# Gate projection of all but the first 272 tokens moved into the attention, between the heads

## The chip, the cores and the metric

The kernel runs on one core of a Trainium2 chip. The metric is the device time of one execution in microseconds (us), as the median of several runs. The core has five engines that run side by side and wait for each other by semaphores: TensorE (PE; PEld is its loading of weights, which lies beside its matmuls), VectorE (DVE), ScalarE (ACT), GpSimd (POOL) and SyncE (SP, whose queue issues nearly all transfers here, one after another in order).

## What is computed

Two layers over 2064 tokens (16 learned meta tokens, then 2048), width 1024. The change lies in the first, a sliding-window attention; the second, a gated DeltaNet, is untouched by it. Of the first:

```python
def attention_mixer(h, norm_w, w_in, q_norm_w, k_norm_w, sinks, w_out):
    u = rms_norm(h, norm_w) @ w_in
    q, k, v, gate = jnp.split(u, [ATTN_WIDTH, ATTN_WIDTH + ATTN_KV_WIDTH, ATTN_WIDTH + 2 * ATTN_KV_WIDTH], axis=-1)
    ...
    o = banded_sink_attention(q, k, v, sinks)
    return (o * jax.nn.silu(gate)) @ w_out
```

q has 16 heads of 64, k and v two; the gate has 1024 columns. A query sees the 128 latest keys, the meta tokens and a sink.

## The kernel before

All matmuls of the first layer run in the float32r format on operands split into a high and a low part, three matmuls for each product (mm3, lines 61 to 63: high by high, low by high, high by low).

**First stage, attn_proj.** The tokens are cut into 17 tiles (16 meta tokens, then 16 of 128). y_tile loads a tile of x, normalises it (norm_rows), transposes it and keeps the parts y_hi and y_lo in SBUF, in five chunks of 400, 384, 384, 384 and 512 tokens. load_w brings 256 columns of w_in and splits them. For q, k and v the tokens are the stationary operand: column blocks 0 and 1 together over all tiles, then 2, 3 and 4 (tile ps_mm). Then hook sets up constants. Then the gate, with the weights stationary and the tokens moving: for each of 8 column tiles of 128 and each chunk 24 matmuls into ps_g, a Silu on ACT (line 231), and a store to the DRAM tensor gate. q and kv go to DRAM too.

**Second stage, attention.** It goes by slots: slot j is a tile t and a group hg of four heads. scores(t, hg) makes s_ps (lines 393, 394), adds the distance table and takes the maximum on DVE (line 395), Exp on ACT (line 405), and scales on POOL. values(t, hg) follows four slots later: it transposes the meta part (tm) and the band (pt), splits them (ph on ACT, pl on DVE, line 444), multiplies by v (pv), multiplies by the gate on POOL (line 461) and splits into oh and ol. finish(t) multiplies by w_out (ps_o), adds x on DVE (line 476) and stores h1 (line 477). prep(t + 1) loads q and kv and transposes them (kps, qps).

```python
        for j in range(len(slots) + LAG):
            with tc.high_priority(offset=150 + (1000 if j < 12 else 0)):
                ...
                    scores(t, hg)
            with tc.high_priority(offset=250 + (1000 if j < 12 else 0)):
                ...
                    values(t, hg)
            for _ in range(2):
                next(fin, None) if fin else None
```

The framework orders the instructions of every engine ahead of time: it takes those that it reckons ready, by the order in which the code makes them, and a higher priority counts as if an instruction had been made that much earlier. On the chip every engine then keeps to its order. A pool gives each tag a number of buffers (bufs); a tile waits until the buffer's last reader is done.

**Second layer.** dn_proj begins where the last tiles of h1 are done; then dn_scan.

Of the kernel before, what the change touches and what calls it, by code (L numbers as in the profile page):

```python
# [15 lines left out]
P = 128  # L16
# [17 lines left out]
NV = 16  # L34
CW = 4096
# [71 lines left out]
def attn_proj(tc, a, sc, ident, hook):  # L107

    nc = tc.nc
# [3 lines left out]
    with (  # L113
# [7 lines left out]
        tc.tile_pool(name="p1w", reuse_waits="tile", bufs=2) as wp,  # L121
# [89 lines left out]
        for cc in range(2, 5):  # L211
            w = load_w(cc)
            for m, r0, i in tiles:
                qkv_tile([(cc, w)], m, r0)
        hook(tpp)
        for c0 in (5, 7):
            ws = [load_w(c0), load_w(c0 + 1)]
            cols = [(e, ct) for e in range(2) for ct in range(2)]
            if c0 == 5:
                order = [(e, ct, c) for e, ct in cols for c in ych]  # L220
            else:
                order = [(e, ct, ych[4]) for e, ct in cols[:0]] + [(e, ct, c) for c in ych[:4] for e, ct in cols]
                order += [(e, ct, ych[4]) for e, ct in cols[0:]]
            for e, ct, (t0, n, hi, lo) in order:
                wh, wl = ws[e]
                ps = mgp.tile([P, 512], F32, tag="mm", name="ps_g")
                for k in range(KT):
                    mm3(nc, ps[:, :n], wh[:, k, ct * P:(ct + 1) * P], wl[:, k, ct * P:(ct + 1) * P],
                        hi[:, k, :], lo[:, k, :], k == 0, k == KT - 1)
                st = sp.tile([P, 512], F32, tag="st", name="st_g")  # L230
                nc.scalar.activation(st[:, :n], ps[:, :n], AF.Silu)
                nc.sync.dma_start(sc["gate"][(c0 - 5 + e) * 2 + ct, :, t0:t0 + n], st[:, :n])


def attn_consts(tc, a, sc, ident, kp, tpp):
# [4 lines left out]
    for kind in range(3):  # L240
        di = kp.tile([P, 512], I32, tag="tmp", name="dist_i")
# [48 lines left out]
def attention(tc, a, sc, ident, ac):  # L290
    nc = tc.nc
    v = nc.vector
    with (
        tc.tile_pool(name="p2q", reuse_waits="tile", bufs=2) as lq,
        tc.tile_pool(name="p2s", reuse_waits="tile", bufs=4) as sp,
        tc.tile_pool(name="p2k", reuse_waits="tile", bufs=2) as lk,
        tc.tile_pool(name="p2p", reuse_waits="tile", bufs=5) as lx,
# [7 lines left out]
        tc.tile_pool(name="p2pt", reuse_waits="tile", bufs=2, space=PSUM) as tpp,  # L305
# [18 lines left out]
        def load_wout():  # L324
            for k in range(KT):
                for c in range(2):
                    raw = lk.tile([P, 512], F32, tag="wraw", name="wo_raw")
# [7 lines left out]
        def prep(t):  # L335
# [9 lines left out]
            else:  # L345
                kps = tpp.tile([P, 2, P], F32, tag="tp", bufs=2, name="kps")
                for kvh in range(2):
                    nc.tensor.transpose(kps[:, kvh, :], kv[:, kvh * P:(kvh + 1) * P], ident)
                kwin = lk.tile([P, 4, 272], F32R, tag="kwin", bufs=3, name="kwin")
# [12 lines left out]
            qst = lk.tile([P, AH, P], F32R, tag="qst", name="qst")  # L362
            for half in range(2):
                qps = tpp.tile([P, 4, P], F32, tag="tp", bufs=2, name="qps")
                for j in range(4):
                    nc.tensor.transpose(qps[:, j, :n], qt[:n, (half * 4 + j) * P:(half * 4 + j + 1) * P], ident[:n, :n])
                qv = qst[:, half * 8:half * 8 + 8, :].rearrange("p (j e) q -> p j e q", e=2)
# [6 lines left out]
            gt = lp.tile([P, KT, P], F32, tag="gate", bufs=1, name="gate_t")  # L374
            nc.sync.dma_start(gt[:, :, :n], sc["gate"][:, :, r0:r0 + n].rearrange("k p t -> p k t"))
            ctx[t] = dict(n=n, i=i, r0=r0, qst=qst, kwin=kwin, vt=vt, gt=gt)
            yield

        def scores(t, hg):
# [6 lines left out]
            for hh in range(4):  # L386
# [5 lines left out]
                q = c["qst"][:, hg * 4 + hh, :n]  # L392
# [27 lines left out]
        def values(t, hg):  # L420
# [4 lines left out]
            tm = tpp.tile([P, P], F32, tag="tp", bufs=2, name="tm")  # L425
# [28 lines left out]
            if hg == 0:  # L454
                c["xt"] = xp.tile([P, D], F32, tag="x", name="x_t")
                nc.sync.dma_start(c["xt"][:n], x_rows(a, i))
                c["oh"] = lp.tile([P, KT, P], F32R, tag="oh", name="oh")
                c["ol"] = lp.tile([P, KT, P], F32R, tag="ol", name="ol")
            ks = slice(hg * 2, hg * 2 + 2)
            oh, ol = c["oh"][:, ks, :n], c["ol"][:, ks, :n]  # L460
            nc.gpsimd.tensor_tensor(ot[:, :, :n], ot[:, :, :n], c["gt"][:, ks, :n], op=ALU.mult)
# [3 lines left out]
        def finish(t):  # L465

            c = ctx[t]
            n, r0, oh, ol, xt = c["n"], c["r0"], c["oh"], c["ol"], c["xt"]
            for cc in range(2):
                cs = slice(cc * 512, cc * 512 + 512)  # L470
                ps = pp.tile([P, 512], F32, tag="o", bufs=1, name="ps_o")
# [4 lines left out]
                v.tensor_tensor(xt[:n, cs], ps[:n], xt[:n, cs], op=ALU.add)  # L476
            (nc.gpsimd if t >= NXT else nc.sync).dma_start(sc["h1"][r0:r0 + n, :], xt[:n])
            yield

# [13 lines left out]
        LAG = 4  # L493
        for j in range(len(slots) + LAG):
            with tc.high_priority(offset=150 + (1000 if j < 12 else 0)):
# [9 lines left out]
            with tc.high_priority(offset=250 + (1000 if j < 12 else 0)):  # L505
# [8 lines left out]
            for _ in range(2):  # L514
                next(fin, None) if fin else None
        for _ in fin:
# [3 lines left out]
def dn_consts(tc, a, kp, ident, psum):  # L520
# [29 lines left out]
    nc.gpsimd.dma_start(nw, a["dn_norm_w"][0].rearrange("(k p) -> p k", p=P))  # L550
    cwr = kp.tile([P, P], F32, tag="cw_raw", name="cw_raw")
    nc.gpsimd.dma_start(cwr, a["dn_conv_w"][0].rearrange("k (t p) -> (k t) p", p=P))
# [8 lines left out]
    for h in range(2):  # L561
        b = slice(h * 64, h * 64 + 64)
        nc.gpsimd.dma_start(nA[b], a["dn_a_log"][0][h::2].unsqueeze(0).to_broadcast([64, 8]))
        nc.gpsimd.dma_start(dtb[b], a["dn_dt_bias"][0][h::2].unsqueeze(0).to_broadcast([64, 8]))
# [696 lines left out]
def body(tc, a, out, upto=9, dbg=None):  # L1261
    nc = tc.nc
    with (
# [7 lines left out]
        def dt(name, shape):  # L1271
# [66 lines left out]
```

## Time and profile before

| | us |
|---|---|
| median of 3 runs | 3198.64 |
| lowest and highest | 3197.79, 3203.32 |
| profiled execution | 3194.22 |
| its span in the trace | 3192.2 |

The trace is of one execution, so sums of its rows are held against 3194.22, of which 3192.2 is the span and 2.0 lies around it. Times within the span are counted from its start. A matmul's duration in the trace holds its pipeline's fill too, so PE's pace is read from the starts of matmuls that follow each other. In a row of a group, the last part is the idle time of the engine just before its instructions, with what ended most of it.

### The profile page before, as it was taken

Reading aid. Unit: us, or ns where it says so; the run is one execution under the profiler, and the core shown is the slowest. Engines: PE = TensorE matmul, PEld = TensorE weight load, DVE = VectorE, ACT = ScalarE, POOL = GpSimd, SP = SyncE. Lnnn points to the kernel's source line nnn. Section 1 sums busy time; section 2 is a strip of 40 time slices with the busy share of each in tenths; the row PEclk is TensorE's granted clock in tenths of the full one; section 3 lists DMA queues with packets and bytes.
Section 4 is the critical chain, followed back from the end, with each engine's and each line's share of the span. In section 5 each row is a group of like instructions: output and inputs, shape, how many; then the busy total and the mean of one; then the engine's idle time right before and its main releaser. Section 6 shows DMA issues by size and latency. Waiting matters only on the chain.

```text
span 3192.2 us, 54290 instructions
## 1 busy us (share of the span) xinstructions
PE 2988.6 (94%) x18685; PEld 2634.1 (83%) x18685; DVE 2228.9 (70%) x6092; ACT 1489.8 (47%) x4247; POOL 968.8 (30%) x1118
## 2 busy tenths in 40 slices
PE   7999998988888999988999999999999999999899
PEld 6999996766666999988999999989986777777687
DVE  6785029999897767896744777987238777788632
ACT  5414147776665444353323544342246665566421
POOL 3001004555453332231111323222145444444100
PEclk9999999999999999999999999999999999999999
DMA  5323123222223353545543444366555666555442
GB/s 120 102 67 98 62 83 95 74 81 65 72 71 102 88 131 92 138 111 144 158 120 80 111 124 124 98 156 186 131 151 159 182 184 177 170 172 163 155 139 99
DMA packets 553596, 385.92 MB, mean 121 GB/s; under 512 B 245513, under 2 KB 505353, under 8 KB 546153
## 3 DMA queue, kind: packets, MB, share of 16 engines
q1 hardware_dynamic: 517032, 365.05, 40.4%
q10 hardware_dynamic: 35952, 16.80, 1.9%
q0 software_dynamic: 336, 0.60, 0.4%
q8 instruction: 148, 2.42, 0.3%
q14 instruction: 128, 1.04, 0.1%
HBM read 245.38 MB, written 136.97 MB: 120 GB/s over the span
## 4 chain that ended last, share of the span: by engine, by line
PE 59%; DVE 23%; ACT 6%; DMA 6%; issue 4%; POOL 1%; SPq 1%; ACTq 0%; DVEq 0%; POOLq 0%
PE ps_d L61 6%; PE ps_d L63 6%; PE ps_d L62 6%; PE ps_o L61 4%; PE ps_o L62 4%; PE ps_o L63 4%; DVE acc L769 3%; PE r_ps L1150 3%; PE ds_ps L1177 3%; PE ps_mm L63 2%; PE ps_mm L61 2%; PE ps_mm L62 2%; DVE Xt L936 2%; PE o_ps L1181 2%; PE vn_ps L1166 2%
## 5 line engine op out<-in xcount | busy, mean ns | idle before, releaser
L61 PE MATMUL ps_d<-y_hi,wi_hi 128*128 128x384 f32 (+2 forms) x2304 | 755.3, 328 | 37.0 <-ACT u L761 30.8
L62 PE MATMUL ps_d<-y_lo,wi_hi 128*128 128x384 f32 (+2 forms) x2304 | 743.8, 323 | 0.0
L63 PE MATMUL ps_d<-y_hi,wi_lo 128*128 128x384 f32 (+2 forms) x2304 | 743.7, 323 | 0.0
L61 PEld LDWEIGHTS ps_d<-y_hi,wi_hi 128*128 128x128 f32 x2304 | 441.0, 191 | 52.1 <-ACT u L761 36.1
L63 PEld LDWEIGHTS ps_d<-y_hi,wi_lo 128*128 128x128 f32 x2304 | 440.9, 191 | 3.5 <-issue 3.3
L62 PEld LDWEIGHTS ps_d<-y_lo,wi_hi 128*128 128x128 f32 x2304 | 441.0, 191 | 3.2 <-issue 2.9
L640 POOL TENSOR_TENSOR wi_raw<-wi_raw,nw 128x1024 f32<-128x1024 f32 x96 | 211.1, 2199 | 685.2 <-DMA wi_raw<-in_dn_w_in 519.9
L769 DVE SCALAR_TENSOR_TENSOR acc<-u,cw,acc 128x1040 f32<-128x1040 f32 (+1 forms) x192 | 291.7, 1519 | 6.1
L57 DVE TENSOR_TENSOR wi_lo<-wi_raw,wi_hi 128x1024 fp32r<-128x1024 f32 x96 | 120.2, 1252 | 206.1 <-ACT wi_hi L56 187.3
L1152 POOL TENSOR_TENSOR S<-S,eL 128x256 f32<-128x256 f32 x248 | 157.2, 643 | 192.3 <-PE r_ps L1150 132.8
L61 PE MATMUL ps_o<-wo,oh 128*128 128x512 f32 x512 | 208.8, 408 | 3.7 <-ACT oh L56 2.9
L63 PE MATMUL ps_o<-wo,ol 128*128 128x512 f32 x512 | 204.1, 399 | 0.0
L1159 ACT ACTIVATE qs<-r_ps,ea 64x128 f32<-64x128 f32 x512 | 182.8, 363 | 44.3 <-DVE xp L1157 34.2
L62 PE MATMUL ps_o<-wo,oh 128*128 128x512 f32 x512 | 202.7, 396 | 0.0
L63 PE MATMUL ps_mm<-w_hi,y_lo 128*128 128x256 f32 (+1 forms) x680 | 192.5, 286 | 4.9 <-DVE y_lo L104 4.8
L61 PE MATMUL ps_mm<-w_hi,y_hi 128*128 128x256 f32 (+1 forms) x680 | 192.9, 286 | 3.0 <-DVE st L190 2.4
L1157 DVE SCALAR_TENSOR_TENSOR xp<-r_ps,c,bv_t 64x128 f32<-64x128 f32 x512 | 174.6, 343 | 27.6 <-ACT qs L1159 10.8
L761 ACT COPY u<-ps_d 128x384 f32<-128x384 f32 (+2 forms) x192 | 84.9, 442 | 232.1 <-PE ps_d L63 231.7
L62 PE MATMUL ps_mm<-w_lo,y_hi 128*128 128x256 f32 (+1 forms) x680 | 192.5, 285 | 0.0
L1150 PE MATMUL r_ps<-S,kq_t 128*128 128x256 f32 x512 | 160.5, 401 | 3.9 <-ACT qs L1159 3.5
L405 ACT ACTIVATE p<-p,nb 128x272 f32<-128x272 f32 (+2 forms) x272 | 134.0, 495 | 51.1 <-DVE nb L400 50.6
L56 ACT CAST wi_hi<-wi_raw 128x1024 fp32r<-128x1024 f32 x96 | 100.5, 1047 | 122.5 <-PE ps_d L62 101.5
(311 smaller groups left out, 7146.5 us busy)
## 6 DMA issues: line engine op xcount, KB each, us to landing
wi_raw<-in_dn_w_in SPq DMA_DIRECT2D x96, 512.0 KB, 4.1
kq_t<-d_kq SPq DMA_DIRECT2D x33, 512.0 KB, 5.3
bv_t<-d_bv SPq DMA_DIRECT2D x33, 512.0 KB, 5.2
x_t<-in_x SPq DMA_DIRECT2D x32, 512.0 KB, 3.7
d_kq<-kq SPq DMA_DIRECT2D x16, 1024.0 KB, 5.4
d_bv<-bv SPq DMA_DIRECT2D x32, 512.0 KB, 4.9
kt_t<-d_ktok SPq DMA_DIRECT2D x64, 256.0 KB, 4.1
z_t<-d_z SPq DMA_DIRECT2D x16, 1024.0 KB, 8.2
```

The lines of the kernel that those rows point to most:

```text
L56: nc.scalar.copy(hi, src)
L57: nc.vector.tensor_tensor(lo, src, hi.bitcast(F32), op=ALU.subtract)
L61: nc.tensor.matmul(ps, lhsT=lh, rhs=rh, start=start, stop=False)
L62: nc.tensor.matmul(ps, lhsT=lh, rhs=rl, start=False, stop=False)
L63: nc.tensor.matmul(ps, lhsT=ll, rhs=rh, start=False, stop=stop)
L405: nc.scalar.activation(p4[:n, hh, k0:272], p4[:n, hh, k0:272], AF.Exp, bias=nb[:n, hh:hh + 1], scale=SLOPES[hg * 4 + hh], accum_out=z[:n, ...
L640: nc.gpsimd.tensor_tensor(raw, raw, nw.unsqueeze(2).to_broadcast([P, KT, P]), op=ALU.mult)
L769: v.scalar_tensor_tensor(acc[:, :ncol], in0=u[:, j:j + ncol], scalar=cw[:, ct, j:j + 1], in1=acc[:, :ncol], op0=ALU.mult, op1=ALU.add)
L1150: nc.tensor.matmul(r, lhsT=kq[:, g, :], rhs=S[:, g], start=True, stop=True)
L1152: nc.gpsimd.tensor_tensor(S[:, g], S[:, g], pers["eL"][hf][:, :, g, n].unsqueeze(2).to_broadcast([P, 2, P]), op=ALU.mult)
L1157: v.scalar_tensor_tensor(xp[hb[h]], in0=r[0:64, h, :], scalar=pers["c1"][hf][hb[h], g, n:n + 1], in1=bv[hb[h], g, :], op0=ALU.mult, op1=AL ...
L1159: nc.scalar.activation(qs[hb[h]], r[64:128, h, :], AF.Copy, scale=pers["ea"][hf][hb[h], g, n:n + 1])
```

## The change

The gate of the first 272 tokens (the meta tile and two more) stays in the first stage (gate_first), between the column blocks, which are taken in the order 2, 5, 3, 6, 4, 7, 8. For the other 1792 tokens, the parts of the normalised tokens (gy) and of the gate's weights (gw) are stored to DRAM in the first stage. In the attention a generator, gates, works through 56 units (7 chunks of 256 tokens by 8 column tiles) of two halves of 12 matmuls, loads gw (512 KB a half) and gy (1 MB a half chunk) from DRAM two halves ahead, takes a Silu and stores the gate. The loop takes its steps between the slots, at the plain priority. To make room, the transposes have one PSUM buffer instead of two, and other tiles shrink or lose a buffer: the gate is loaded for each slot, x and h1 in halves of 512 columns. The small constants' loads of the second layer go from POOL's queue to SP's.

```diff
@@ y_tile
             norm_rows(nc, sp, xp, xt, m)
             transpose_split(nc, tpp, ident, xt, m, hi, lo, c0)
+            if r0 >= G0:
+                ci, off = divmod(r0 - G0, GN)
+                for hl, y in enumerate((hi, lo)):
+                    nc.sync.dma_start(sc["gy"][ci, :, :, hl, :, off:off + m],
+                                      y[:, :, c0:c0 + m].bitcast(F32).rearrange("p (h k) t -> p h k t", h=2))
@@ attn_proj, behind the first pass (wp has bufs=3 in place of 2)
-        for cc in range(2, 5):
-            w = load_w(cc)
-            for m, r0, i in tiles:
-                qkv_tile([(cc, w)], m, r0)
-        hook(tpp)
-        for c0 in (5, 7):
-            ws = [load_w(c0), load_w(c0 + 1)]
...
+        def gate_first(e, w):
+            wh, wl = w
+            hi, lo = at[0][:2]
+            for ct in range(2):
+                cs = slice(ct * P, ct * P + P)
+                for hl, x in enumerate((wh, wl)):
+                    nc.sync.dma_start(sc["gw"][e * 2 + ct, :, :, hl],
+                                      x[:, :, cs].bitcast(F32).rearrange("p (h k) c -> p h k c", h=2))
                 ps = mgp.tile([P, 512], F32, tag="mm", name="ps_g")
                 for k in range(KT):
+                    mm3(nc, ps[:, :G0], wh[:, k, cs], wl[:, k, cs], hi[:, k, 0:G0], lo[:, k, 0:G0], k == 0, k == KT - 1)
...
+        order = [2, 5, 3, 6, 4, 7, 8]
+        ws = {}
+        for j, cc in enumerate(order):
+            for c in order[j:j + 2]:
+                if c not in ws:
+                    ws[c] = load_w(c)
+            if cc < 5:
+                for m, r0, i in tiles:
+                    qkv_tile([(cc, ws[cc])], m, r0)
+                if cc == 4:
+                    hook(tpp)
+            else:
+                gate_first(cc - 5, ws[cc])
@@ attention
+        tc.tile_pool(name="p2g", reuse_waits="tile", bufs=3) as gyp,
-        tc.tile_pool(name="p2pt", reuse_waits="tile", bufs=2, space=PSUM) as tpp,
+        tc.tile_pool(name="p2pt", reuse_waits="tile", bufs=1, space=PSUM) as tpp,
...
+        def gates():
+            units = [(ci, ct) for ci in range(NGC) for ct in range(KT)]
+            ys, wts = {}, {}
+            gps = pp.tile([P, 2, GN], F32, tag="g", bufs=1, name="ps_g")
+            for u, (ci, ct) in enumerate(units):
+                ps = gps[:, u % 2, :]
+                for kh in range(2):
+                    nu = u * 2 + kh
+                    for w in (nu, nu + 1, nu + 2):
+                        if w // 2 < len(units) and w not in wts:
+                            c2, t2 = units[w // 2]
+                            y = (c2, w % 2)
+                            if y not in ys:
+                                ys[y] = gyp.tile([P, 2, 4, GN], F32R, tag="gy", name="gy")
+                                nc.sync.dma_start(ys[y].bitcast(F32), sc["gy"][c2, :, w % 2])
+                            wts[w] = gyp.tile([P, 2, 4, P], F32R, tag="gw", name="gw")
+                            nc.sync.dma_start(wts[w].bitcast(F32), sc["gw"][t2, :, w % 2])
+                    y, w = ys[ci, kh], wts.pop(nu)
+                    for k in range(4):
+                        mm3(nc, ps, w[:, 0, k], w[:, 1, k], y[:, 0, k], y[:, 1, k], kh + k == 0, kh + k == 4)
+                        if k == 1:
+                            yield
+                    if kh == 0:
+                        yield
+                st = gyp.tile([P, GN], F32, tag="st", bufs=2, name="st_g")
+                nc.scalar.activation(st, ps, AF.Silu)
+                t0 = G0 + ci * GN
+                nc.sync.dma_start(sc["gate"][ct, :, t0:t0 + GN], st)
+                yield
@@ the loop over slots (offsets 200 and 330 in place of 150 and 250)
+        filler, gdone = gates(), 0
...
+            while gdone * (len(slots) - 7) < NGC * KT * 4 * (j + 1) and next(filler, 1) is None:
+                gdone += 1
```

How the order of the instructions changes, at three places. On PE, around a tm (the transposes of the meta part) in the middle of the attention, before:

```order
L61 MATMUL ps_o<-wo_hi_6032,oh 128x512
L62 MATMUL ps_o<-wo_lo_6033,oh 128x512
L426 MATMUL tm<-ident,px 128x128
L63 MATMUL ps_o<-wo_hi_6032,ol 128x512
L61 MATMUL ps_o<-wo_hi_6034,oh 128x512
L62 MATMUL ps_o<-wo_lo_6035,oh 128x512
L63 MATMUL ps_o<-wo_hi_6034,ol 128x512
L440 MATMUL pt<-ident,p_8598 128x128 x4
```

and at such a place with the change (ps_g is the gate, whose matmuls go on below the rows shown):

```order
L64 MATMUL ps_o<-wo_hi_5183,oh 128x512
L65 MATMUL ps_o<-wo_lo_5184,oh 128x512
L66 MATMUL ps_o<-wo_hi_5183,ol 128x512
L446 MATMUL tm<-ident,px 128x128
L460 MATMUL pt<-ident,p_6960 128x128 x4
L64 MATMUL ps_g<-gy,gw 128x256
L65 MATMUL ps_g<-gy,gw 128x256
L66 MATMUL ps_g<-gy,gw 128x256
L64 MATMUL ps_g<-gy,gw 128x256
```

Runs of 12 or 24 matmuls of the gate now stand between the attention's own. On ACT, around Exp (p), before:

```order
L405 ACTIVATE p_9278,z<-p_9278,nb 128x272 x4
L407 ACTIVATE es<-es 128x4
L433 CAST mt<-tm 32x128
L370 CAST qst<-qps 64x4x128
L443 CAST ph<-pt 128x512
L462 CAST oh<-ot 128x256
L443 CAST ph<-pt 128x512
L405 ACTIVATE p_9384,z<-p_9384,nb 128x272 x4
```

and with the change (L526 is the Silu of the gate):

```order
L424 ACTIVATE es<-es 128x4
L526 ACT_TABLE_LOAD
L526 ACTIVATE st_g<-ps_g 128x256
L471 COPY ob<-pv 64x512
L389 CAST qst<-qps 64x4x128 x2
L479 CAST oh<-ot 128x256
L526 ACTIVATE st_g<-ps_g 128x256
L463 CAST ph<-pt 128x512 x2
L422 ACT_TABLE_LOAD
L422 ACTIVATE p_8004,z<-p_8004,nb 128x272 x4
```

A table load now stands at each change between Silu and Exp. In SP's queue, one tile's transfers in the attention before:

```order
L338 DMA q_t<-d_q 128x1024
L477 DMA d_h_68<-x_t 128x1024
L456 DMA x_t<-in_x 128x1024
L341 DMA kv_t<-d_kv 128x384
L375 DMA gate_t<-d_gate 128x8x128
```

and part of one tile's with the change:

```order
L517 DMA gw<-d_gw 128x1024
L496 DMA d_h_70<-x_t 128x512
L528 DMA d_gate<-st_g 128x256
L489 DMA x_t<-in_x 128x512
L517 DMA gw<-d_gw 128x1024
L496 DMA d_h_70<-x_t 128x512
L444 DMA gate_t<-d_gate 128x2x128
L517 DMA gw<-d_gw 128x1024
L489 DMA x_t<-in_x 128x512
L528 DMA d_gate<-st_g 128x256
```

The loads of gw stand behind stores of the gate (d_gate) and of h1 (d_h) in one queue.

## Rows read from the trace of the kernel before

**Rows 1.** Stretches from:to (us), length, busy us per engine, granted clock, DMA share, GB/s.

```profile
0.00:294.00 294.00, 266.91 (x2180) 260.36 (x2180) 227.22 (x1215) 118.32 (x306) 42.99 (x121) 0.98 0.33 94
294.00:484.00 190.00, 188.85 (x1059) 178.58 (x1060) 33.35 (x140) 61.79 (x155) 16.10 (x29) 1.00 0.25 80
484.00:999.00 515.00, 448.73 (x2323) 352.82 (x2322) 460.36 (x1426) 354.12 (x1077) 263.55 (x369) 0.97 0.26 80
1100.00:1300.00 200.00, 193.18 (x1281) 185.68 (x1280) 144.29 (x242) 83.01 (x226) 60.95 (x58) 0.99 0.48 122
1800.00:2000.00 200.00, 199.15 (x1345) 191.20 (x1344) 155.95 (x244) 94.19 (x238) 59.32 (x39) 1.00 0.48 126
```

**Rows 2.** DVE's groups, 484 to 999 us: count, busy us, mean ns, idle before.

```profile
L395 DVE CUSTOM_DVE_ANT_0 p<-s_ps,tab 128x272 f32<-128x272 f32 (+1 forms) x248 | 102.9, 430 | 10.5 <-PE s_ps L394 7.1 <-POOL vt L360 0.5
...
L57 DVE TENSOR_TENSOR wo_lo<-wo_raw,wo_hi 128x512 fp32r<-128x512 f32 x12 | 8.5, 706 | 1.2 <-ACT wo_hi L56 1.2
L352 DVE SCALAR_TENSOR_TENSOR kwin<-kps,wkk,kwin 128x256 fp32r<-128x256 f32 x13 | 6.3, 482 | 0.3
```

**Rows 3.** Waits, 484 to 999 us: total us, times, longest.

```profile
ACT p L405 <- DVE nb L400: 50.6, 32, 5.9
...
PEld s_ps L393 <- DVE mx L395: 27.0, 46, 1.5
```

**Rows 4.** Line L476 over the span: count, durations ns, first and last start, forms.

```profile
L476 DVE TENSOR_TENSOR x_t<-ps_o,x_t x34: 660/683/694, 517.3 to 999.1; 128x512 f32<-128x512 f32 x32, 16x512 f32<-16x512 f32 x2
```

**Rows 5.** Tile ps_g over the span: count, durations ns, first and last start, forms.

```profile
L61 PE MATMUL ps_g<-y_hi,w_hi x320: 333/334/440, 294.0 to 481.0; 128*128 128x384 f32 x96, 128*128 128x400 f32 x32, 128*128 128x512 f32 x32
...
L231 ACT ACTIVATE st_g<-ps_g x40: 491/492/602, 303.5 to 483.2; 128x384 f32<-128x384 f32 x24, 128x400 f32<-128x400 f32 x8, 128x512 f32<-128x512 f32 x8
```

**Rows 6.** PE's timeline, projection of q, k, v: start, duration.

```profile
239.77 0.28 PE L63 MATMUL ps_mm<-w_hi,y_lo 128*128 128x256 f32 x1
...
242.89 0.28 PE L62 MATMUL ps_mm<-w_lo,y_hi 128*128 128x256 f32 x1
```

**Rows 7.** PE's timeline, gate projection.

```profile
329.82 0.33 PE L62 MATMUL ps_g<-y_lo,w_hi 128*128 128x384 f32 x1
...
333.99 0.33 PE L62 MATMUL ps_g<-y_lo,w_hi 128*128 128x384 f32 x1
```

**Rows 8.** Waits, 0 to 110 us.

```profile
PE tp L101 <- ACT x_t L90: 19.2, 3, 10.7
```

**Rows 9.** PE's timeline inside the attention.

```profile
724.42 0.40 PE L63 MATMUL ps_o<-wo_hi,ol 128*128 128x512 f32 x1
...
727.86 0.39 PE L63 MATMUL ps_o<-wo_hi,ol 128*128 128x512 f32 x1
...
729.60 0.60 PE L440 MATMUL pt<-ident,p 128*128 128x128 f32 x4
729.96 0.37 PE L393 MATMUL s_ps<-kwin,qst 128*128 128x272 f32 x1
730.17 0.29 PE L394 MATMUL s_ps<-kwin,qst 128*128 128x272 f32 x1
```

**Rows 10.** ACT's timeline at a change of function.

```profile
476.98 0.16 ACT L433 CAST mt<-tm 32x16 fp32r<-32x16 f32 x1 [0.23 <-DVE mt L431]
477.16 1.28 ACT L405 ACT_TABLE_LOAD   x1
478.46 0.41 ACT L405 ACTIVATE p<-p,nb 128x144 f32<-128x144 f32 x1
```

**Rows 11.** Readers of tile tm: count, durations ns, first and last start.

```profile
L433 ACT CAST mt<-tm x136: 145/256/262, 457.3 to 979.9; 32x128 fp32r<-32x128 f32 x128, 32x16 fp32r<-32x16 f32 x8
```

**Rows 12.** DMA issues: count, KB each, median us from issue to landing.

```profile
kq_t<-d_kq SPq DMA_DIRECT2D x33, 512.0 KB, 5.3
```

**Rows 13.** Waits of SP's own queue, 484 to 999 us.

```profile
SPq L477 <- DVE x_t L476: 140.6, 10, 19.7
```

More of the change, by code (lines that the diff above doesn't have):

```diff
@@ L34 @@
 NV = 16
+GN = 256
+G0 = NMETA + GN
+NGC = (L - G0) // GN
 CW = 4096
@@ L240, in attn_consts @@
     for kind in range(3):
-        di = kp.tile([P, 512], I32, tag="tmp", name="dist_i")
+        di = kp.tile([P, 272], I32, tag="tmp", name="dist_i")
         mb = {0: 1 << 14, 1: NMETA, 2: 0}[kind]
@@ L326, in load_wout @@
                 for c in range(2):
-                    raw = lk.tile([P, 512], F32, tag="wraw", name="wo_raw")
+                    raw = gyp.tile([P, 512], F32, tag="gw", name="wo_raw")
                     cs = slice(c * 512, c * 512 + 512)
@@ L361, in prep @@
             yield
-            qst = lk.tile([P, AH, P], F32R, tag="qst", name="qst")
+            qst = []
             for half in range(2):
-                qps = tpp.tile([P, 4, P], F32, tag="tp", bufs=2, name="qps")
+                qh = lk.tile([P, 8, P], F32R, tag="qst", bufs=3, name="qst")
+                qst.append(qh)
+                qps = tpp.tile([P, 4, P], F32, tag="tp", name="qps")
                 for j in range(4):
                     nc.tensor.transpose(qps[:, j, :n], qt[:n, (half * 4 + j) * P:(half * 4 + j + 1) * P], ident[:n, :n])
-                qv = qst[:, half * 8:half * 8 + 8, :].rearrange("p (j e) q -> p j e q", e=2)
+                qv = qh.rearrange("p (j e) q -> p j e q", e=2)
                 for e in range(2):
@@ L373, in prep @@
                     yield
-            gt = lp.tile([P, KT, P], F32, tag="gate", bufs=1, name="gate_t")
-            nc.sync.dma_start(gt[:, :, :n], sc["gate"][:, :, r0:r0 + n].rearrange("k p t -> p k t"))
-            ctx[t] = dict(n=n, i=i, r0=r0, qst=qst, kwin=kwin, vt=vt, gt=gt)
+            ctx[t] = dict(n=n, i=i, r0=r0, qst=qst, kwin=kwin, vt=vt)
             yield
@@ L424, in values @@
             p4, px = c.pop(("p", hg))
-            tm = tpp.tile([P, P], F32, tag="tp", bufs=2, name="tm")
+            ks = slice(hg * 2, hg * 2 + 2)
+            gt = lp.tile([P, 2, P], F32, tag="gate", bufs=3, name="gate_t")
+            nc.sync.dma_start(gt[:, :, :n], sc["gate"][ks, :, c["r0"]:c["r0"] + n].rearrange("k p t -> p k t"))
+            tm = tpp.tile([P, P], F32, tag="tp", name="tm")
             nc.tensor.transpose(tm[:, :n], px[:n].rearrange("p h e m -> p (h e m)").bitcast(F32), ident[:n, :n])
@@ L504, in attention @@
                     next(pre, None) if pre and hg == 0 else None
-            with tc.high_priority(offset=250 + (1000 if j < 12 else 0)):
+            with tc.high_priority(offset=330 + (1000 if j < 12 else 0)):
                 if j >= LAG:
@@ L1269, in body, with dt @@
         sc = {}
-        def dt(name, shape):
-            sc[name] = (dbg or {}).get(name) if dbg and name in dbg else dp.tile(list(shape), F32, name="d_" + name)
+        def dt(name, shape, dtype=F32):
+            sc[name] = (dbg or {}).get(name) if dbg and name in dbg else dp.tile(list(shape), dtype, name="d_" + name)
         dt("q", (L, D))
```

49 lines of the change are left out of this document (20 added, 29 removed).

## The prediction

> **What bounds the kernel now.** I first cut the span at the places where the work changes [rows 1]. From 0 to 294 us the projection of q, k and v runs, and PE's weight loads, which run one after another when PE never waits, fill 260 of 294 us. From 294 to 484 us the gate projection runs: PE is full (189 of 190 us), DVE has 33 us of work. From 484 to 999 us the attention runs the other way round: DVE is busy 460 of 515 us, weight loads only 353. So one stretch wants PE and leaves DVE idle, the next wants DVE and leaves PE idle, and they follow each other. DVE's groups in the attention [rows 2] are many and small; ten of them, from the first row shown to the last, belong to scores and prep (300 us by their sum), four more to values and finish (197 us): 60 to 40. The waits there end at DVE too: ACT waits 51 us for nb, PE's loads 27 us for mx [rows 3]. The pace is read from the addition of x in finish [rows 4]: two a tile, 34 of them between 517.3 and 999.1 us, so 29.2 us a tile and 7.3 us for one slot (a tile and four heads). By 60 to 40 a slot's scores cost 4.4 us at this pace, its values 2.9.
>
> **The change, step by step.** All sums are PE's rates at full clock against the profiled execution (3194.2 us; the median of the runs is 4.4 us above).
>
> *What leaves the first stage.* The gate has 40 accumulations, 24 of 384 columns, 8 of 400, 8 of 512 [rows 5], of 24 matmuls each. Back to back, 256 columns take 0.120 us (26 steps from 239.77 to 242.89) [rows 6], 384 take 0.174 (24 steps from 329.82 to 333.99) [rows 7], so 0.00042 us a column. The gate's 960 matmuls are then 178 us of PE, of a stretch of 190.
>
> *What stays there.* 8 accumulations of 272 columns: 192 matmuls at 0.127, 24 us. Two new things stand in SP's queue during the projection: stores of gy and gw between the loads of x, and six small loads at the very start. In the first 110 us PE already waits 19.2 us for the normalised x [rows 8]; a doubling is the upper bound, nothing the lower, and I take 6, since the loads of x still go out two or three tiles ahead. Scores begin at 294 + 24 + 6 = 324 us.
>
> *What the attention gets.* 7 chunks by 8 column tiles by 24 are 1344 matmuls of 256 columns, 161 us. So PE's work in all grows by about 7 us; the gain can only come from overlap.
>
> *How much overlaps.* The order of the program says where. Ahead of the first moved matmul stand 70 of the 544 matmuls of scores and 2 of the 68 transposes tm; between the first and the last stand 318 and 40; behind the last 156 and 26. So there are three parts.
>
> Part one, without cover, 8.75 slots of scores, of which four are the meta tile's with 16 rows. DVE's share: the splits of w_out, 11 us (16 of 0.706 us [rows 2]), 4.75 slots by 4.4, four small ones at about 2.5, and the two small values, 3: 45 us. Lower bound 25 (PE's own need), upper 64 (8.75 slots at 7.3).
>
> Part two. Inside the attention 512 columns take 0.229 us (15 steps from 724.42 to 727.86), four transposes 0.36 and 0.09 more for the next matmul behind them [rows 9]; the 272 columns of scores cost 0.127 as above. The attention's own 480 ps_o, 318 s_ps, 184 pv and 424 transposes then take 110 + 40 + 42 + 48 = 240 us, with the moved ones 401. DVE needs 40 slots by 7.3 = 292 us in it, so PE becomes the bound. ACT has 354 us over about 64 slots [rows 1], 220 for 40 slots; to it come 56 Silu of 256 columns (0.38 us by the 384 and 512 columns of rows 5) and a table load at each change between Exp and Silu, 36 and 37 in the order, at 1.28 us [rows 10]: 220 + 22 + 92 = 334 us. PE's own efficiency where it is the bound I take from two stretches of the next stage, where weight loads fill 93% and 96% [rows 1]: 95%, so 401 / 0.95 = 422 us. Lower bound 401. Upper bound: the present attention has 792 ps_o, 500 s_ps, 313 pv and 698 transposes behind the gate, 395 us by the same rates in 515, a share of 77%, which gives 401 / 0.77 = 521.
>
> Part three, again bound by DVE: 19.5 slots of scores by 4.4 and 26 of values by 2.9 are 161 us, then the tail from the last tm copy at 979.9 [rows 11] to the last addition's end at 999.8, 20 us: 181. The single buffer for transposes (two before) is part of this estimate; since pv already waits for the copies of tm that free it, I add nothing.
>
> *Sum.* 324 + 45 + 422 + 181 = 972 us against 999.8 for the attention's end now. Behind it nothing is changed. 28 us less: 3166 for the profiled execution, 3171 for the median.
>
> *A rule against it.* At the change of function ACT's copy ends at 477.14, the load starts at 477.16 and Exp at 478.46 [rows 10]: 1.28 us and no gap. The Trainium skill (ScalarE: Activation LUTs, "What ACT_TABLE_LOAD costs") puts a drain of about 1380 ns to each load and says to group calls by table set, which this change does the opposite of. By that figure 72 loads would add an estimated 99 us to ACT. Here no drain is visible, so the sum goes by the row; the case in which a switch costs double is a rival below.
>
> **The rivals.**
>
> *Gate operands come late (slower).* A half projection (12 matmuls) needs a 512 KB gw from DRAM, with three buffers. PE asks for one every 422 / 112 = 3.8 us, so a buffer may take 11.3 us round: 5.3 us landing, as the 512 KB loads of kq take [rows 12], 0.4 to issue and up to 3.8 of use leave 1.8 us for waiting in SP's queue. Each gw of a next column tile stands behind the store of a Silu, itself behind a table load of 1.28; and SP stands up to 19.7 us at one wait for the addition of x, 140.6 us in ten [rows 13]. From a mean wait of 1.8 us this decides. At 3 us a round is 12.5 us, 112 / 3 of them 467 us, 45 more: 17 over now, 3216. For it: one queue, in order. Against: 292 and 334 us of DVE and ACT in 422 let their answers come early, so the queue waits mostly for PE itself.
>
> *ACT pays twice for a switch, or the start-up is as slow as its bound (same).* Another 92 us make ACT 426, at 95% 448, 26 more than part two: 3197. Start-up at 64 and the first stage at 12: 25 more, 3196.
>
> *The attention keeps its 77%.* If answers of DVE and ACT stay as close behind PE as now, part two lasts 521 us: 3270. Against it stands DVE's slack of 130 us.
>
> *More than forecast.* Part two without loss, start-up at 25: 41 less, 3130.
>
> **How the numbers follow.** Within 0.2% is 6.4 us, about what a measurement of this kernel can tell from no change. Forecast, with the terms inside their nearer bounds (3140 to 3190): 0.50, faster. More than forecast: 0.07, faster. Switch or start-up: 0.15, same. Late operands: 0.22, slower. 77%: 0.06, slower. That is 0.57, 0.15 and 0.28. The range from 3130 to 3230 leaves out the last case, the worst of the late operands and half of "more": under 0.2.
>
> **What would show it.** Right: the first stage's end near 324 us, a stretch of some 420 us with weight loads over 90% and DVE near 70%, then one of 180 us like the present attention, dn_proj some 28 us earlier. Late operands: PE waiting for gw by tens of us, and SP's waits behind stores of st_g. Switches: 70 loads and ACT over 90% busy. Wrong altogether if PE's waits for DVE or ACT inside part two stay above 60 us, or if the projection of q, k, v itself grows by over 20 us.

## The result, and the profile after

The changed kernel takes 3282.85 us (median of 4 runs, 3278.21 to 3299.1), the kernel before 3200.98 (4 runs, 3197.79 to 3205.93): a ratio of 1.0263, interval 1.0223 to 1.0304. It is slower by 82 us, where I had forecast 28 us faster. The profiled execution took 3287.34 us.

The attention's end (the last addition of x) is the best place to compare: the work behind it is the same everywhere, but its time ran from 2175 to 2203 us in the traces below. It stood at 999.8 us [rows 4]. Line L495 of the changed kernel is the same addition:

```profile
L495 DVE TENSOR_TENSOR x_t<-ps_o,x_t x34: 669/691/693, 405.3 to 1087.6; 128x512 f32<-128x512 f32 x32, 16x512 f32<-16x512 f32 x2
```

It now ends at 1088.3, 88.5 us later. The moved matmuls give the cuts between my parts (line L64 of tile ps_g, first and last start):

```profile
L64 PE MATMUL ps_g<-gy,gw x448: 277/283/583, 373.0 to 847.6; 128*128 128x256 f32 x150
```

The changed kernel's stretches, cut there, with the columns of [rows 1]:

```profile
0.00:330.20 330.20, 299.95 (x2374) 291.23 (x2375) 240.95 (x1245) 131.57 (x340) 50.10 (x127) 0.96 0.55 166
330.20:373.00 42.80, 24.18 (x118) 17.98 (x117) 34.20 (x153) 30.52 (x111) 12.53 (x26) 0.56 0.69 228
373.00:847.90 474.90, 425.64 (x2750) 375.14 (x2751) 275.20 (x855) 319.15 (x774) 163.21 (x228) 0.97 0.64 209
847.90:1088.30 240.40, 195.04 (x909) 150.47 (x907) 177.61 (x540) 135.98 (x403) 97.51 (x136) 0.89 0.23 70
```

| | forecast, us | measured, us | off by |
|---|---|---|---|
| first stage, to the first scores | 324 | 330.2 | +6 |
| part one, uncovered | 45 | 42.8 | -2 |
| part two, moved matmuls | 422 | 474.9 | +53 |
| part three, no moved matmuls | 181 | 240.4 | +59 |
| end of the attention | 972 | 1088.3 | +116 |

The first two terms hold. In part two no engine is full: weight loads fill 79%, DVE 58%, ACT 67%. In part three DVE, which I took for the bound, fills 74%, where it filled 89% before [rows 1].

The waits of part two (373 to 848 us) of the changed kernel, total us, times, longest:

```profile
POOL px L430 <- PE tm L446: 67.1, 32, 5.5
...
PEld ps_g L64 <- ACT st_g L526: 41.4, 26, 4.1
PE ps_g L64 <- ACT st_g L526: 33.7, 25, 3.6
...
PE ps_g L64 <- DMA gw<-d_gw: 6.6, 5, 2.5
```

Two things are new. TensorE waits 75 us (51 times for 56 units) for a Silu before a unit may begin. And GpSimd, about to write px, waits 67 us for tm to have read an older px; before the change that wait was 0.2 us over 484 to 999 us:

```profile
POOL px L413 <- PE tm L426: 0.2, 1, 0.2
```

TensorE hardly waits for the operands from DRAM, which land as fast as the kernel's other 512 KB loads (3.9 to 6.0 us; count, KB, median us):

```profile
gw<-d_gw SPq DMA_DIRECT2D x112, 512.0 KB, 4.7
```

One of these waits, on TensorE's timeline and on ACT's (start, duration, in brackets the idle time and what ended it):

```profile
568.26 0.28 PE L66 MATMUL ps_g<-gy,gw 128*128 128x256 f32 x1
...
569.11 0.28 PE L411 MATMUL s_ps<-kwin,qst 128*128 128x272 f32 x1
570.35 0.38 PE L64 MATMUL ps_g<-gy,gw 128*128 128x256 f32 x1 [0.95 <-ACT st_g L526]
```

```profile
568.62 1.28 ACT L526 ACT_TABLE_LOAD   x1 [3.69 <-PE ps_g L66]
569.91 0.38 ACT L526 ACTIVATE st_g<-ps_g 128x256 f32<-128x256 f32 x1
```

A unit's last matmul starts at 568.26. Its table load begins only then, at 568.62, though ACT had been idle for 3.69 us. The Silu ends at 570.29, and the next unit, which writes the other half of ps_g, starts at 570.35. The two halves lie in one PSUM bank and did not act as two buffers.

### The profile page after: what moved, and what is told of

The parts are those of the page before. It is cut to its first block, busy times and chain, and to the rows that moved or that the text cites. A ratio compares the mean times of both kernels' runs of the same rounds, so it can differ in the third digit from the quotient of the medians.

```text
span 3285.6 us, 56150 instructions
## 1 busy us (share of the span) xinstructions
PE 3033.2 (92%) x19261; PEld 2679.7 (82%) x19261; DVE 2236.5 (68%) x6092; ACT 1573.7 (48%) x4335; POOL 965.3 (29%) x1111
## 4 chain that ended last, share of the span: by engine, by line
PE 58%; DVE 19%; ACT 10%; DMA 7%; issue 4%; POOL 1%; SPq 1%; ACTq 0%; DVEq 0%; POOLq 0%
PE ps_d L64 6%; PE ps_d L66 6%; PE ps_d L65 6%; PE ps_o L64 5%; PE ps_o L66 4%; PE ps_o L65 4%; DVE acc L823 3%; PE r_ps L1204 3%; PE ds_ps L1231 2%; ACT p L422 2%; DVE X L992 2%; PE ps_mm L64 2%; DVE Xt L990 2%; PE ps_mm L65 2%; PE ps_mm L66 2%
## 5 line engine op out<-in xcount | busy, mean ns | idle before, releaser
L64 PE MATMUL ps_d<-y_hi,wi_hi 128*128 128x384 f32 (+2 forms) x2304 | 755.3, 328 | 30.4 <-ACT u L815 23.7
L64 PEld LDWEIGHTS ps_d<-y_hi,wi_hi 128*128 128x128 f32 x2304 | 441.2, 191 | 45.2 <-ACT u L815 28.3
L64 PE MATMUL ps_mm<-w_hi,y_hi 128*128 128x256 f32 (+1 forms) x680 | 197.1, 292 | 16.9 <-ACT y_hi L106 12.7
L64 PE MATMUL ps_o<-wo,oh 128*128 128x512 f32 x512 | 208.8, 408 | 3.8 <-ACT oh L59 2.9
L64 PE MATMUL ps_g<-gy,gw 128*128 128x256 f32 x448 | 135.2, 302 | 40.4 <-ACT st_g L526 33.7
L433 POOL TENSOR_TENSOR p<-p,z 128x1024 f32<-128x1024 f32 (+1 forms) x64 | 117.9, 1842 | 161.2 <-DVE z L426 93.1
```

The lines of the kernel that those rows point to most:

```text
L64: nc.tensor.matmul(ps, lhsT=lh, rhs=rh, start=start, stop=False)
L433: nc.gpsimd.tensor_tensor(p4[:n, :, k0:256], p4[:n, :, k0:256], z[:n].unsqueeze(2).to_broadcast([n, 4, 256 - k0]), op=ALU.mult)
```

## The experiments

The theory: the loss is the single transpose buffer, and the table loads that hold ps_g's bank. The rivals: the operands from DRAM, ACT's work as such, the other cuts. Each run stands beside one of the kernel before on the same chip. These are single runs but for the changed kernel (4 and 4), e13 and e14 (10 each, beside 19), and those 19 of one kernel on one chip spread from 3191.8 to 3218.1 us, so a difference of some 25 us between single runs says little by itself. The last column is free of what happens behind the attention, but not of the first stage, whose end lay up to 10 us apart where no edit touched it.

| run | us | before beside it | difference | end of attention |
|---|---|---|---|---|
| changed kernel | 3282.9 | 3201.0 | +82 | 1088.3 |
| e3_before_tp1 | 3305.5 | 3212.9 | +93 | 1111.0 |
| e4_before_cuts | 3316.5 | 3212.9 | +104 | 1121.5 |
| e15_tp1_more_px | 3286.8 | 3200.9 | +86 | 1093.1 |
| e16_tm_apart | 3202.9 | 3200.9 | +2 | 1018.2 |
| e7_before_pt1 | 3321.0 | 3192.5 | +129 | 1117.7 |
| e6_after_pt1 | 3314.2 | 3192.5 | +122 | 1108.9 |
| e1_copy | 3230.9 | 3212.9 | +18 | 1034.0 |
| e2_dve_evac | 3263.0 | 3212.9 | +50 | 1065.1 |
| e5_tanh | 3238.7 | 3192.5 | +46 | 1041.3 |
| e9_one_half | 3286.4 | 3211.5 | +75 | 1091.2 |
| e8_share_tanh | 3192.8 | 3192.5 | 0 | 1016.1 |
| e10_share_tanh_one_tp | 3247.0 | 3211.5 | +35 | 1045.7 |
| e11_share_silu | 3252.1 | 3211.5 | +41 | 1052.7 |
| e12_share_pool_store | 3201.0 | 3211.5 | -11 | 1000.0 |
| e13_early | 3199.3 | 3201.8 | -2 | 1014.1 |
| e14_early_pool_store | 3190.0 | 3201.8 | -12 | 995.8 |

### The transpose buffer

e3 is the kernel before with one edit; e4 has all the attention's cuts, offsets and queues of the change, but no moved gate.

```diff
-        tc.tile_pool(name="p2pt", reuse_waits="tile", bufs=2, space=PSUM) as tpp,
+        tc.tile_pool(name="p2pt", reuse_waits="tile", bufs=1, space=PSUM) as tpp,
```

> The kernel before with one PSUM buffer for transposes (tm, qps, kps) in place of two, nothing else. Buffer theory (part three, which took 243 us where 181 were forecast, is slow because of this buffer): a slot takes 8.3 us or more in place of 7.3, the time is 3255 us or more. Rival, the buffer is hidden: 3195 to 3210 us.

> The kernel before with all that the change does inside the attention apart from the moved projection: one buffer for transposes, kwin 2 and qst in halves, gate loaded for each slot, x and h1 in halves, offsets 200 and 330, constants loaded by SP; the gate projection as before in the first stage. If the cuts slow part three: 3255 us or more, and more than with the one buffer alone if the other cuts count. If part three is slow only through the order that the moved matmuls leave behind, or the clock: 3195 to 3215.

The buffer alone costs 111 us at the attention's end, without any moved gate, and brings the new wait (484 to 1000 us of e3):

```profile
POOL px L413 <- PE tm L426: 61.2, 36, 3.9
```

A part of the 111 is not the buffer's. The gate's last matmuls in the first stage, which neither edit touches, began at 481.0 us before [rows 5], in e3 and in e4 at

```profile
L61 PE MATMUL ps_g<-y_hi,w_hi x320: 333/335/522, 299.9 to 487.9; 128*128 128x384 f32 x96, 128*128 128x400 f32 x32, 128*128 128x512 f32 x32
```

```profile
L64 PE MATMUL ps_g<-y_hi,w_hi x320: 333/335/501, 292.1 to 478.2; 128*128 128x384 f32 x96, 128*128 128x400 f32 x32, 128*128 128x512 f32 x32
```

Counted from there the buffer costs 104 us, and the other cuts add 20. From e4 to the changed kernel, that is by moving the gate itself, the end comes 33 us earlier, and what paid for its bank lost three times that. That the 33 are near the 28 that I had forecast is luck: they are what the table loads leave of 87 (e1 below), and beside an attention slower than the one I reckoned with.

Every edit of a buffer also lets the framework order the instructions anew: e3's first tm starts at 488.25 us, that of the kernel before at 448.66. So these runs price a buffer together with the order that comes with it.

How one buffer costs so much was open until the last two runs. e15 is e3 with px in seven buffers in place of five; e16 keeps both banks but gives one to tm alone and one to the transposes of q and k.

```diff
-            tm = tpp.tile([P, P], F32, tag="tp", name="tm")
+            tm = tpp.tile([P, P], F32, tag="tm", name="tm")
```

> The kernel before with one transpose buffer (3305.5 us when it ran) and px in seven buffers in place of five. In that run GpSimd waits 61 to 71 us for a tm to free a buffer of px, against less than 1 us in the kernel before. If the loss goes by way of px (late tm, so no px, so no scaling of the next heads): 3250 us or less. If the late tm itself is the loss, with px only a sign of it: 3290 us or more.

> The kernel before with its two transpose banks kept, but dealt out: one for tm alone, one for the transposes of q and k, so that neither can take both. If the loss with one buffer comes from tm standing behind the slow transposes of q and k (four copies of 0.6 to 0.7 us each): 3190 to 3230 us, like the kernel before. If tm needs two buffers for itself: 3270 us or more.

The pace shows it. These are the starts of one tile's first tm and that of the tile nine further on (tiles 5 and 14); first the kernel before, then e3, e15 and e16:

```profile
614.09 0.30 PE L426 MATMUL tm<-ident,px 128*128 128x128 f32 x1 [2.23 <-DVE mt L431]
906.23 0.27 PE L426 MATMUL tm<-ident,px 128*128 128x128 f32 x1
```

```profile
674.11 0.27 PE L426 MATMUL tm<-ident,px 128*128 128x128 f32 x1
1017.47 0.27 PE L426 MATMUL tm<-ident,px 128*128 128x128 f32 x1
```

```profile
667.69 0.27 PE L426 MATMUL tm<-ident,px 128*128 128x128 f32 x1
997.34 0.27 PE L426 MATMUL tm<-ident,px 128*128 128x128 f32 x1
```

```profile
633.93 0.33 PE L426 MATMUL tm<-ident,px 128*128 128x128 f32 x1
926.09 0.33 PE L426 MATMUL tm<-ident,px 128*128 128x128 f32 x1 [1.61 <-DVE mt L431]
```

A tile takes 32.5 us before, 38.2 with one buffer, 36.6 with more px, and 32.5 again when tm has a bank of its own. So tm does not need two buffers for itself; it must not queue with the transposes of q and k, whose four copies take 0.58 (ACT) and 0.69 us (DVE) each. The px wait is mostly a sign of it: in e15 it is gone, and the time, 3286.8 us, lies between the two expectations and close to the second. The pace explains half of e3's loss, 51 us in these nine tiles; 60 were lost ahead of tile 5 (674.11 against 614.09), 7 of them in the first stage. e16's attention ends 18 us later than that of the kernel before, all of it lost ahead of tile 5 (633.93). Its total is only 2 us above the run beside it because the work behind the attention took 9 us less in that execution, and the run beside it 7 us more than the profiled one. Why the start is slower I did not take apart.

What I had not looked at is the clock. The nine tiles of the kernel before and of e3, with the columns of [rows 1]:

```profile
614.09:906.23 292.14, 256.16 (x1344) 203.75 (x1345) 265.10 (x799) 197.46 (x602) 152.17 (x210) 0.98 0.24 75
```

```profile
674.11:1017.47 343.36, 274.49 (x1320) 216.45 (x1319) 259.84 (x783) 193.99 (x596) 150.31 (x206) 0.89 0.19 60
```

TensorE's granted clock is 0.98 in the one and 0.89 in the other, and the same work keeps it busy for 274 us in place of 256. So up to 18 of the 51 us may go with the clock; the other 33 are time in which TensorE stands idle. The clock is low in e15 (0.91 over its nine tiles) and e4 (0.90) too, and hardly in e16 (0.96). No run holds the clock fixed, so its share is not shown.

e7 and e6 ask whether any bank would do: pt's two tiles in one bank, in the kernel before (its freed bank left empty) and in the changed kernel (two transpose buffers again).

```diff
-            for (b0, vt), ptp in zip(blocks, (pt0, pt1)):
+            for (b0, vt), ptp in zip(blocks, (pt0, pt0)):
```

> The kernel before with pt's two tiles in one bank, nothing else changed, and the bank left empty: the price of the bank that the run before this one takes. Theory of the single transpose buffer: pt is read by one copy and one subtraction and costs little, 3200 to 3225 us. Rival (any bank costs as much as the transposes' second one): 3290 us or more.

> The changed kernel with two transpose buffers again; the bank comes from pt, whose two tiles then take turns in one. Theory of the single transpose buffer (it sets 38 us a tile in the part without moved matmuls, where the kernel before took 32.6): that part falls from 241 us towards 190, the time to 3220 to 3240 us. Rival (it is the other cuts, or any bank that is taken from the attention costs the same): 3280 us or more, tiles still 38 us apart.

Here my theory fell: both runs meet the rival, and pt's second bank is worth even more (118 us at the attention's end) than the transposes'. The single transpose buffer is not special; the pace rests on each of these two pairs, and the change had no free bank to take.

### The Silu and its bank

e1 takes Copy in place of the moved Silu, which leaves that function out, so that no table changes; e2 copies ps_g to SBUF on DVE and takes the Silu from there; e9 uses one half of ps_g's bank for every unit.

```diff
-                nc.scalar.activation(st, ps, AF.Silu)
+                nc.scalar.activation(st, ps, AF.Copy)                # e1
...
+                v.tensor_copy(st, ps)                                # e2
+                nc.scalar.activation(st, st, AF.Silu)
...
-                ps = gps[:, u % 2, :]
+                ps = gps[:, 0, :]                                    # e9
```

> The changed kernel with Copy in place of Silu for the 1792 tokens' gate: this part of the computation is left out, and with it 72 table loads; the order on PE stays the same, row by row. Bank theory (each unit's first matmul waits for ACT to have read the unit before, because both halves of ps_g lie in one bank, and the table load of 1.28 us stands ahead of that read): 51 waits lose about 1.28 us each, so the stretch of the moved matmuls falls from 475 to about 410 us and the time to some 3215 us. Rival, the gate operands (gw) set the pace: the stretch stays above 465 us and the time above 3270.

> The changed kernel, but DVE copies ps_g to SBUF and ACT takes the Silu from there; all table loads stay, DVE gets 56 copies of about 0.35 us. Bank theory: PE waits only for DVE's copy, the waits of ps_g for st_g (75 us) fall to 20 or less, the stretch from 475 to about 420, the time to some 3230 us. Rival, ACT's sheer work with 72 loads slows the attention's own chain: waits move to ph and oh, and the time stays above 3265.

> The changed kernel with every unit of moved matmuls in the first half of ps_g's bank, so that the second half is never used and a unit must wait for the Silu of the unit ahead of it by address too. Theory of the bank (the two halves never worked as two buffers, a unit waits for the Silu ahead of it anyway): 3270 to 3300 us, the same as the changed kernel, part two 475 us. Rival (the halves do hide a part of the Silu): 3300 us or more.

e1's parts two and three, with the columns of [rows 1]:

```profile
371.00:798.30 427.30, 411.17 (x2752) 368.74 (x2753) 278.58 (x856) 227.13 (x704) 163.74 (x228) 0.99 0.70 233
798.30:1034.00 235.70, 192.40 (x907) 148.03 (x905) 176.14 (x539) 133.34 (x401) 96.55 (x135) 0.90 0.23 71
```

Without the table loads part two takes 427 us (forecast 422; expected of e1, about 410) and TensorE waits 10 us for st_g in place of 75; part three is untouched. e2 shows which half of the cost is which. With the loads left on ACT but off the bank, TensorE's wait for the reader falls to 12 us. Part two takes 441 us, but holds 95 matmuls less than in the changed kernel, and part three 252. Over both parts the changed kernel takes 715 us, e2 693 and e1 663: of the 52 us, 22 go with the bank that is held during load and Silu, 30 with the loads on ACT and the copies that DVE got. So e2's total stands between both expectations. e9 is as slow as the changed kernel: the second half of the bank never helped. The Trainium skill (PSUM — Partial Sum Buffer, "PSUM bank collisions raise a hardware error") says accesses must be guarded by bank (strictly, by bank and group of 32 partitions), since another engine there collides even at other addresses. I had not drawn on it; by it, ps_g was one buffer from the start, and e9 agrees (3286.4 against 3282.9 us). In the code ps_g is also one tile, and no run makes two of it, so whether the framework set the wait for the bank or for the tile is not shown.

e5 makes the same function without a table change: gate weights halved once, tanh(h) on ACT, (tanh(h) + 1) * h on DVE.

```diff
-                nc.scalar.activation(st, ps, AF.Silu)
+                nc.scalar.activation(st, ps, AF.Tanh)
+                v.scalar_tensor_tensor(st, in0=st, scalar=1.0, in1=ps, op0=ALU.add, op1=ALU.mult)
```

> The changed kernel, whole computation, with Silu in the attention replaced by Tanh: the gate weights are halved once (h = x/2), ScalarE takes tanh(h), VectorE makes (tanh(h)+1)*h, which is the same function. Theory of the table loads (a Silu between two Exps costs two loads of 1.28 us and holds the bank of the next unit while they run): as the run with Copy, 3231 us, plus up to 0.3 us for the second reader of each of 56 units, so 3230 to 3250 us, with part two near 430 us. Rival (the gain of the run with Copy came from leaving the Silu out, not the loads): 3263 us or more.

Its time lies in the theory's range; beside its own run of the kernel before it stands 28 us worse than e1, by the attention's end 7. The table loads in the stages of the changed kernel from 294 to 1120 us (count, busy us, mean ns) were 73, and e5 has one of them left, for the first Exp:

```profile
L422 ACT ACT_TABLE_LOAD x37 | 47.5, 1283 | 1.0 <-DVE nb L417 0.4
L526 ACT ACT_TABLE_LOAD x36 | 46.2, 1283 | 10.2 <-issue 4.9 <-PE ps_g L66 4.8
```

The attention ends 47 us earlier than in the changed kernel.

### Both mended

e8 gives the transposes their second bank back without taking one from pt: ps_g and ps_o share a bank in turn, each unit and each half of finish written out whole, with e5's Tanh. e10 is e8 with one transpose buffer, e11 is e8 with Silu.

```diff
-            gps = pp.tile([P, 2, GN], F32, tag="g", bufs=1, name="ps_g")
...
-                ps = gps[:, u % 2, :]
+                ps = pp.tile([P, 512], F32, tag="o", bufs=1, name="ps_g")[:, :GN]
...
-            for _ in range(2):
+            if (j - LAG) % 2:
                 next(fin, None) if fin else None
```

> The changed kernel with Tanh as above, two transpose buffers, pt in its two banks, and ps_g and ps_o in turn in one bank, each unit and each half of the output projection written out whole. The moved matmuls then reach through almost the whole attention. By the theories of the table loads and of the transpose buffer together: scores from 330 us, 43 us up to the first moved matmul, 511 us of matmul work at 95 per cent, 50 us behind it, so the end of the attention near 960 us and 3160 us in all. Rival (the shared bank makes every unit and half wait about 1 us for its reader, 90 in all): 3250 us.

> The version with Tanh and with ps_g and ps_o in one bank (3192.8 us), but with a single transpose buffer, and the bank that this frees left empty. Theory of the transposes: the second buffer is worth about 90 us where nothing hides it and less under moved matmuls, so 3235 to 3290 us. Rival (under moved matmuls the attention's own chain has slack, so the second buffer is worth little here): 3190 to 3210 us.

> The version with ps_g and ps_o in one bank and two transpose buffers, but with Silu as in the changed kernel. Theory of the table loads: 56 units, each with a load of 1.28 us ahead of its Silu and most with one behind it, while the one bank waits: 3192.8 plus 45 to 60, so 3235 to 3255 us. Rival (other loads or orders hide them): 3200 us or less.

e8 takes 3192.8 us, level with the kernel before and not the 3160 that I expected. Even that is partly luck: its attention ends 16 us later than that of the kernel before, and the work behind it, which is the same, took 2175 us in this execution against 2192. Ten runs of e13 below, whose attention in the trace ends within 2 us of e8's, are level too. Its stretches: first stage, uncovered start, moved matmuls, rest.

```profile
0.00:329.50 329.50, 299.46 (x2381) 290.75 (x2381) 239.99 (x1248) 131.39 (x342) 49.23 (x129) 0.97 0.56 168
329.50:373.90 44.40, 29.07 (x132) 22.63 (x132) 38.66 (x183) 36.91 (x136) 14.94 (x32) 0.56 0.70 232
373.90:959.10 585.20, 543.36 (x3402) 476.20 (x3403) 433.35 (x1327) 334.25 (x1020) 242.55 (x335) 0.97 0.56 183
959.10:1016.10 57.00, 50.63 (x246) 40.84 (x246) 33.40 (x111) 25.19 (x64) 18.18 (x24) 0.98 0.56 174
```

The third took 585 us for 511 of matmul work by the forecast's rates, 87% in place of 95%. Against it, one transpose buffer costs 30 us more at the attention's end (e10) and Silu 37 (e11); both totals lie in their expected ranges. The buffer's price under cover is under a third of the 104 without. My reading, which no run tests, is that the moved matmuls fill TensorE's time while tm is late. The wait is there all the same (372 to 1000 us of e10; e8 has no such row):

```profile
POOL px L433 <- PE tm L449: 87.7, 43, 4.7
```

### What is left

In e8 TensorE still waits 21 us for gw, and the first moved matmul stands 44 us behind the first scores. e12 is e8 with the h1 stores issued by GpSimd; e13 is e8 with load_wout moved from ahead of the slots to slot 4; e14 has both.

```diff
-                nc.sync.dma_start(sc["h1"][r0:r0 + n, cs], xt[:n])
+                nc.gpsimd.dma_start(sc["h1"][r0:r0 + n, cs], xt[:n])   # e12, e14
...
-        load_wout()
...
         for j in range(len(slots) + LAG):
+            if j == 4:                                                 # e13, e14
+                load_wout()
```

> The version with Tanh and the shared bank (3192.8 us), its stores of h1 issued by GpSimd in place of SyncE. In that version SyncE waits 133 us for x_t ahead of these stores, the loads of gw stand behind it, and TensorE waits 21 us for gw. If the queue is the cause: 3170 to 3185 us. If GpSimd's own work is then late (it waits for x_t in its place): 3190 us or more.

> The version with Tanh, the shared bank and two transpose buffers, with the load of the output weights moved from ahead of the slots to slot 4: its sixteen raw tiles go through the three buffers of gw, so the first moved matmul stood behind all of them. Theory of the start (43 us in which the attention runs uncovered, TensorE busy 28 of them at 0.56 of its clock, because gw is not there): the first moved matmul starts near 345 in place of 373.9 us, and the attention ends 15 to 25 us earlier: the median 0.5 to 0.8 per cent below the kernel before. Rival (the output weights are then late, and the end of the attention is set by its last tiles): no more than 5 us, equal to the kernel before.

> As the run before it, and the stores of h1 on GpSimd's queue in place of SyncE's. If SyncE's waits for x_t hold up gw (TensorE waits 21 us for gw in the version without either edit): another 5 to 10 us below the run before it. Rival (SyncE has slack now, or GpSimd waits in its place): the same as the run before it within 3 us, or slower.

e13 starts the moved matmuls at 336.8 us and gains nothing: 0.999, interval 0.9969 to 1.001, the attention's end 2 us earlier than in e8. Work done early was not the work that was late. The stores are. e12's single run, 3201.0 us, lies in the range of its rival, and only its trace speaks for the stores: the attention ends 16 us earlier than in e8, and TensorE's waits for gw from 372 to 1000 us fall from 21 to 6. e14 settles it with ten runs: 3189.99 us against the 3199.29 of e13, 9 us for the stores alone, with 7 us of waits for gw. It is 0.9968 of the kernel before (3201.76 us), interval 0.9946 to 0.9991, and the one version that beats both kernels, by 0.3%. e14's stretch with moved matmuls:

```profile
333.50:937.80 604.30, 560.63 (x3497) 486.93 (x3498) 471.38 (x1468) 364.48 (x1142) 272.04 (x392) 0.96 0.58 191
```

## Why the prediction was wrong

Two steps failed. The first is "The single buffer for transposes (two before) is part of this estimate; since pv already waits for the copies of tm that free it, I add nothing." I looked only at tm's own readers. The buffer is shared with the transposes of q and k, and tm queues behind their copies (e3, e16). Under moved matmuls that costs some 30 us (e10 against e8), in an attention without them 104 (e3). In part three three tiles of the changed kernel take 39.0 us each, where a tile took 32.5 before:

```profile
874.07 0.27 PE L446 MATMUL tm<-ident,px 128*128 128x128 f32 x1
991.00 0.27 PE L446 MATMUL tm<-ident,px 128*128 128x128 f32 x1
```

The second is "220 + 22 + 92 = 334 us" on ACT, which I took as covered because it stayed below PE's 422. Without the Silu and its loads the attention ends 54 us earlier (e1), of the 88 us that were lost; these loads stood on TensorE's path.

Of part three's 59 us not all is the change's. The last 156 matmuls of scores to the attention's end, before and with the change (540 of the 544 matmuls are in the first trace):

```profile
799.16:999.80 200.64, 175.53 (x892) 139.67 (x893) 171.48 (x526) 130.93 (x388) 97.74 (x134) 0.97 0.25 81
```

```profile
851.13:1088.30 237.17, 193.06 (x897) 149.03 (x895) 174.76 (x534) 134.67 (x402) 96.63 (x135) 0.88 0.23 70
```

The kernel before needs 201 us for what I had put at 181. So some 20 of the 59 are a reading of mine: the 29.2 us a tile from the additions of x [rows 4] include the quick tiles at the end, where in the middle, by tm, a tile took 32.5. The other 36 or so came with the buffer and the other cuts, and TensorE's matmuls, at a clock of 0.88 for 0.97, fill 17.5 us of them. So the buffer put at nothing cost part three no more than about 36 us.

Point by point:

- **Part two, 422 us: off by 53.** The mechanism (TensorE bound, 95%) was right for the work as I counted it: e1 takes 427. My 92 us for table loads was added to ACT's total and called covered, since ACT stayed below 422; the total is right (334 forecast, 319 measured) and beside the point. A load stands between a unit's end and the next unit's start at 36 of 56 units, because ps_g was in truth one buffer. The 75 us of waits are past the 60 that I had named as the sign against me.
- **The rule on table loads.** ACT's load again took 1.28 us, with the Silu 0.01 us behind it. As before no drain is visible, so the size of a switch was right and its place was wrong.
- **First stage and part one**: 330.2 for 324 and 42.8 for 45, both inside their bounds.
- **Late operands**, my rival for slower: no. gw lands in 4.7 us, and TensorE waits 11 us for it in part two.
- **ACT pays twice, or a slow start**: no, neither. **The attention keeps its 77%**: part two came to 401 of 475, 84%, by a cause that this rival did not name.
- **The gain from overlap**: there, 33 us from e4 to the changed kernel, and 87 to e1. That it can't be had whole shows in e8: with both waits mended, the first stage (329.5 us) and the uncovered start cost what I had summed, and the covered stretch reaches 87%.

Not settled: what holds that stretch at 87%, beyond the queue of stores; why pt's second bank is worth 118 us; and how much of each buffer's price is the lower clock.

## What to carry to other kernels

When a change takes a buffer away, price it like any edit: list every tile that takes turns in that buffer, and ask which of them is late for another's readers, not only for its own. Count PSUM buffers by bank: the two halves of one bank were one buffer here, and everything between the last matmul of one tile and its reader's end, a table load too, is then on the path of the next. And run the payment alone: e3, one edit of the kernel before, shows a loss larger than that of the whole change, without the move. Look at the granted clock of such a run too.

## What was not expected of the hardware

A table load need not run ahead into ACT's idle time. In all five places of the changed kernel where ACT stood idle (0.34 to 3.79 us) in front of a load for a moved Silu, the load began only 0.35 to 0.49 us behind the start of the unit's last matmul, as at 568.62. It is no rule: once, with ACT busy up to the load, it began ahead of the unit's last matmul:

```profile
658.09 1.28 ACT L526 ACT_TABLE_LOAD   x1
...
658.16 0.28 PE L66 MATMUL ps_g<-gy,gw 128*128 128x256 f32 x1
...
658.52 0.28 PE L66 MATMUL ps_g<-gy,gw 128*128 128x256 f32 x1
```

TensorE's granted clock, a mean of its levels of 1.2 and 2.4 GHz, was 0.56 in part one, where matmuls fill 24 of 43 us, 0.89 in part three (195 of 240) and 0.97 in part two (426 of 475): of these three, the less of a stretch the matmuls filled, the lower its clock.
